# Grouped instance norm: stores of two units, gamma spread in small copies, and 1/std times gamma on ScalarE

## The chip, the cores and the metric

The kernel runs on one core of a Trainium2 chip. The metric is device time in microseconds (us). Before the change it is 626.83 us, the median of three runs (626.78 to 626.91).

## The reference, cut to what matters

```python
def reference(x, gamma):            # x: (4, 8, 16, 256, 256) f32, gamma: (8, 16) f32
    mu = x.mean(axis=(3, 4), keepdims=True)
    var = ((x - mu) ** 2).mean(axis=(3, 4), keepdims=True)
    x_norm = (x - mu) / np.sqrt(var + 1e-5)
    return x_norm * gamma[None, :, :, None, None]
```

Each of the 512 channels (4 x 8 x 16) is normalised over its own 256 x 256 plane and multiplied by one number of gamma. The input is 134.2 MB and the output as much; every byte is read once and written once.

## The kernel before

**Units.** The 512 channels are cut into `U = 32` units of `K = 16` channels. One channel's plane lies on `S = 8` partitions, so a unit is a tile of 128 partitions x 8192 f32: 32 KB on a partition, 4 MB in all. In DRAM a unit is one contiguous piece of 4 MB (`xv[u]`, `ov[u]`). Gamma has 128 numbers, so unit u takes group `u % NG` of `NG = 8` groups of 16.

**Buffers.** There are `AHEAD = 6` slots of 4 MB, each its own tile, which is nearly all of the on-chip memory. A unit is loaded into its slot, normalised in place and stored from it. Unit u+6 takes the slot of unit u, so its load waits until the store of unit u has landed.

**Queues.** The first six loads are issued at once: units 1 and 3 by ScalarE's queue (ACTq), the others by SyncE's (SPq). After that SPq issues every load (L48) and ACTq every store (L129); GpSimd's queue brings gamma's 512 bytes. An instruction waits in its own engine's order: a store issued by ScalarE stands behind ScalarE's work for that unit and ahead of its work for the next.

**Gamma, once.** One VectorE copy (L78) writes gamma, each number 8 times, into a row of 1024 numbers (`g_rep`) on one partition. Eight matmuls with a 1x1 one (L83) turn each 128 of them into a column of PSUM (`g_ps`), and one VectorE copy (L89) brings the 128 x 8 result to `g_col`. All of it stands ahead of unit 0 on VectorE.

**A unit.** The loop is written out by hand and the order on each engine is the order of the text (`manual_schedule`):

- VectorE sums the tile (L102) while ScalarE squares and sums it (L103) into the other half of `st[:, u]`.
- TensorE (L111) adds up the 8 partitions of each channel and gives the negative means to all of them, in PSUM.
- VectorE works out the negative variance (L112); ScalarE takes the root (L116); VectorE takes the reciprocal (L120) and multiplies it by gamma's column (L122).
- VectorE writes `(x - mean) * scale` over the tile (L125).
- ScalarE issues the store (L129), SyncE the load of unit u+6 (L48), which waits for that store.

Of the kernel before, what the change touches and what calls it, by code (L numbers as in the profile page):

```python
# [1 line left out]

# [4 lines left out]

F32 = mybir.dt.float32
U8 = mybir.dt.uint8
ALU = mybir.AluOpType  # L10
ACTF = mybir.ActivationFunctionType
AX = mybir.AxisListType


@with_exitstack
def kernel(
    ctx: ExitStack,
    tc: tile.TileContext,
    x: bass.AP,
    gamma: bass.AP,  # L20
    out: bass.AP,
):
    nc = tc.nc
    B, G, C, H, W = x.shape
    P = nc.NUM_PARTITIONS
    HW = H * W
    n_ch = B * G * C
    S = 8
    K = P // S
    F = HW // S  # L30
    U = n_ch // K
    NG = (G * C) // K
    AHEAD = 6
    assert HW % S == 0 and (G * C) % K == 0

    xv = x.rearrange("b g c h w -> (b g c h w)").rearrange("(u p f) -> u p f", p=P, f=F)
    ov = out.rearrange("b g c h w -> (b g c h w)").rearrange("(u p f) -> u p f", p=P, f=F)
    gv = gamma.rearrange("g c -> (g c)")

    data = ctx.enter_context(tc.tile_pool(name="data", bufs=1))  # L40
    singles = ctx.enter_context(tc.tile_pool(name="singles", bufs=1))
    psum = ctx.enter_context(tc.tile_pool(name="psum", bufs=4, space=bass.MemoryType.PSUM))
    ctx.enter_context(tc.manual_schedule())

    slots = [data.tile([P, F], F32, name=f"xt{i}") for i in range(AHEAD)]

    def load(u, queue):
        queue.dma_start(out=slots[u % AHEAD][:], in_=xv[u])  # L48


    g_row = singles.tile([1, G * C], F32, name="g_row")
    nc.gpsimd.dma_start(out=g_row[:], in_=gv[None, :])  # L52
    for u in range(AHEAD):
        load(u, nc.scalar if u in (1, 3) else nc.sync)


    eps_t = singles.tile([P, 1], F32, name="eps_t")
    nc.gpsimd.memset(eps_t[:], 1e-5)  # L58
    one = singles.tile([1, 1], F32, name="one")
    nc.gpsimd.memset(one[:], 1.0)  # L60
    navg = singles.tile([P, K, S], F32, name="navg")
    nc.gpsimd.memset(navg[:], -1.0 / HW)  # L62
    nc.gpsimd.affine_select(  # L63
        out=navg[:], in_=navg[:], pattern=[[-S, K], [0, S]], compare_op=ALU.is_ge,
        fill=0.0, base=0, channel_multiplier=1,
    )
    nc.gpsimd.affine_select(  # L67
        out=navg[:], in_=navg[:], pattern=[[S, K], [0, S]], compare_op=ALU.is_ge,
        fill=0.0, base=S - 1, channel_multiplier=-1,
    )  # L70
    navg_w = navg[:].rearrange("p k s -> p (k s)")
    root_eps = singles.tile([P, 1], F32, name="root_eps")
    nc.scalar.activation(out=root_eps[:], in_=eps_t[:], func=ACTF.Sqrt)  # L73
    g_rep = singles.tile([1, NG, K, S], F32, name="g_rep")
    g_ps = psum.tile([P, NG], F32, name="g_ps", bufs=1)
    g_col = singles.tile([P, NG], F32, name="g_col")

    nc.vector.tensor_copy(  # L78
        out=g_rep[:],
        in_=g_row[:].rearrange("o (n k) -> o n k", n=NG).unsqueeze(3).to_broadcast([1, NG, K, S]),  # L80
    )
    for n in range(NG):
        nc.tensor.matmul(  # L83
            out=g_ps[:, n : n + 1],
            lhsT=g_rep[:, n].rearrange("o k s -> o (k s)"),
            rhs=one[:],
            start=True, stop=True,
        )
    nc.vector.tensor_copy(out=g_col[:], in_=g_ps[:])  # L89

    junk = singles.tile([P, F], U8, name="junk")

    st = singles.tile([P, U, 2], F32, name="st")
    nvar = singles.tile([P, U], F32, name="nvar")
    std = singles.tile([P, U], F32, name="std")
    rstd = singles.tile([P, U], F32, name="rstd")
    scale = singles.tile([P, U], F32, name="scale")

    squares = []
    for u in range(U):  # L100
        t = slots[u % AHEAD]
        nc.vector.reduce_sum(out=st[:, u, 0:1], in_=t[:], axis=AX.X)  # L102
        square = nc.scalar.activation(  # L103
            out=junk[:], in_=t[:], func=ACTF.Square, accum_out=st[:, u, 1:2],
        )
        if u:

            tc.declare_no_dep(square.ins, squares[-1].ins, reason="junk, ordered by the root between")
        squares.append(square)
        ps = psum.tile([P, 2], F32, name="ps")  # L110
        nc.tensor.matmul(out=ps[:], lhsT=navg_w, rhs=st[:, u], start=True, stop=True)  # L111
        nc.vector.tensor_scalar(  # L112
            out=nvar[:, u : u + 1], in0=ps[:, 0:1], scalar1=ps[:, 0:1],
            scalar2=ps[:, 1:2], op0=ALU.mult, op1=ALU.add,
        )
        nc.scalar.activation(  # L116
            out=std[:, u : u + 1], in_=nvar[:, u : u + 1], func=ACTF.Sqrt,
            bias=eps_t[:], scale=-1.0,
        )
        nc.vector.reciprocal(out=rstd[:, u : u + 1], in_=std[:, u : u + 1])  # L120
        g = u % NG
        nc.vector.tensor_mul(  # L122
            out=scale[:, u : u + 1], in0=rstd[:, u : u + 1], in1=g_col[:, g : g + 1],
        )
        nc.vector.tensor_scalar(  # L125
            out=t[:], in0=t[:], scalar1=ps[:, 0:1], scalar2=scale[:, u : u + 1],
            op0=ALU.add, op1=ALU.mult,
        )
        nc.scalar.dma_start(out=ov[u], in_=t[:])  # L129
        if u + AHEAD < U:  # L130
            load(u + AHEAD, nc.sync)


# [1 line left out]
_INS = ['x', 'gamma']  # L135
_OUTS = [((4, 8, 16, 256, 256), 'float32')]


# [23 lines left out]
```

## Time and profile before

| what | value |
|---|---|
| median of three runs | 626.83 us |
| span of the profiled execution, first to last instruction | 625.2 us |
| around the span (median less span) | 1.6 us |
| bytes moved | 268.46 MB at a mean of 429 GB/s |
| DMA engines' share of the span, both queues (52.9% + 46.8%) | 99.7% |
| VectorE busy | 443.2 us (71%) |
| ScalarE busy | 238.8 us (38%) |
| TensorE busy | 21.4 us (3%) |
| granted TensorE clock | 1.000 |

The profiled execution's own time is its span with what lies around it. No time of its own is listed beside the span, so the median stands for it. Queue q1 holds the loads that SPq issues, q10 all that ACTq issues (two loads and all stores). A DMA packet of x is one row of 32 KB on one of 16 DMA engines; a unit is 8 packets on each engine.

### The profile page before, as it was taken

What the parts mean: (1) busy time and instruction counts of PE and PEld (TensorE: products, weight loads), DVE (VectorE), ACT (ScalarE), POOL (GpSimd) and SP (SyncE); (2) the same over time, 40 slices, a digit from 0 to 9 for tenths busy, and PEclk for the clock granted to TensorE, in tenths of its full rate; (3) what the DMA queues carried; (4) which work ended last, traced back from release to release, by engine and by line L of the source; (5) the groups of instructions that cost most, each with busy time, mean ns of one, the idle gap of its engine ahead of it and who ended that gap; (6) DMA issues with size and microseconds to landing.
All of it is one profiled execution on the core that took longest, in us unless ns stands there. A gap on an engine that the chain in (4) does not pass through costs nothing.

```text
span 625.2 us, 627 instructions
## 1 busy us (share of the span) xinstructions
PE 21.4 (3%) x80; PEld 19.6 (3%) x80; DVE 443.2 (71%) x162; ACT 238.8 (38%) x98; POOL 1.9 (0%) x10
## 2 busy tenths in 40 slices
PE   2000000000000000000000000000000000000000
PEld 2000000000000000000000000000000000000000
DVE  0588999999776687666786767867668676687730
ACT  0444444444443244432344423444224442244400
POOL 1000000000000000000000000000000000000000
DMA  8999999999999999999999999999999999999998
GB/s 369 436 403 436 436 436 436 436 426 432 434 434 436 424 434 436 436 434 436 436 421 434 434 434 432 432 434 436 436 434 436 436 419 434 434 436 432 432 434 369
DMA packets 9251, 268.46 MB, mean 429 GB/s; under 512 B 1057, under 2 KB 1057, under 8 KB 1057
## 3 DMA queue, kind: packets, MB, share of 16 engines
q10 hardware_dynamic: 4896, 142.61, 52.9%
q1 hardware_dynamic: 4320, 125.83, 46.8%
q14 instruction: 3, 0.02, 0.0%
q0 software_dynamic: 32, 0.00, 0.0%
HBM read 134.22 MB, written 134.22 MB: 429 GB/s over the span
## 4 chain that ended last, share of the span: by engine, by line
another core or an unknown queue 61%; DMA 17%; DVE 15%; SPq 1%; PE 1%; issue 0%; ACT 0%
DMA xt<-in_x_dram 10%; DVE st L102 10%; DMA out_dram<-xt 8%; DVE xt L125 5%; SPq L48 1%; PE ps L111 1%; ACT std L116 0%; DVE nvar L112 0%; DVE rstd L120 0%; DVE scale L122 0%
## 5 line engine op out<-in xcount | busy, mean ns | idle before, releaser
L102 DVE TENSOR_REDUCE st<-xt 128x1 f32<-128x8192 f32 x32 | 277.9, 8684 | 105.3 <-DMA xt<-in_x_dram 105.3
L103 ACT ACTIVATE junk<-xt 128x8192 uint8<-128x8192 f32 x32 | 224.9, 7029 | 275.4 <-DMA xt<-in_x_dram 232.2
L125 DVE TENSOR_SCALAR xt<-xt,ps,scale 128x8192 f32<-128x8192 f32 x32 | 145.6, 4550 | 1.2
L116 ACT ACTIVATE std<-nvar,eps_t 128x1 f32<-128x1 f32 x32 | 9.4, 294 | 79.7 <-DVE nvar L112 79.7
L111 PE MATMUL ps<-st,navg 128*128 128x2 f32 x64 | 17.9, 349 | 562.0 <-DVE st L102 562.0
L111 PEld LDWEIGHTS ps<-st,navg 128*128 128x128 f32 x64 | 16.1, 312 | 563.8 <-issue 563.8
L112 DVE TENSOR_SCALAR nvar<-ps 128x1 f32<-128x1 f32 x32 | 9.2, 287 | 23.9 <-PE ps L111 23.9
L120 DVE RECIPROCAL rstd<-std 128x1 f32<-128x1 f32 x32 | 5.3, 164 | 11.6 <-ACT std L116 11.6
L78 DVE COPY g_rep<-g_row 1x1024 f32<-1x1024 f32 x1 | 0.7, 683 | 10.6 <-DMA g_row<-in_gamma_dram 10.6
L103 ACT ACTIVATION_READ_ACCUMULATOR junk<-xt 128x1 f32 x32 | 6.0, 186 | 0.0
L122 DVE TENSOR_TENSOR scale<-rstd,g_col 128x1 f32<-128x1 f32 x32 | 5.1, 159 | 1.1
L83 PE MATMUL g_ps<-one,g_rep 1*128 1x1 f32 x16 | 3.5, 347 | 11.5 <-DVE g_rep L78 11.5
L83 PEld LDWEIGHTS g_ps<-one,g_rep 1*128 1x128 f32 x16 | 3.5, 326 | 11.4 <-issue 11.4
L89 DVE COPY g_col<-g_ps 128x8 f32<-128x8 f32 x1 | 0.2, 167 | 3.7 <-PE g_ps L83 3.7
L73 ACT ACT_TABLE_LOAD x1 | 1.3, 1283 | 1.7 <-PEq L146 1.7
L52 POOL DMA_DIRECT2D g_row<-in_gamma_dram x1 | 0.6, 607 | 0.8 <-POOLq L146 0.8
L63 POOL TENSOR_SCALAR_AFFINE_SELECT navg<-navg 128x128 f32<-128x128 f32 x1 | 0.4, 398 | 0.1
L67 POOL TENSOR_SCALAR_AFFINE_SELECT navg<-navg 128x128 f32<-128x128 f32 x1 | 0.4, 398 | 0.1
L62 POOL MEMSET navg<- 128x128 f32 x1 | 0.2, 230 | 0.0
L73 ACT ACTIVATE root_eps<-eps_t 128x1 f32<-128x1 f32 x1 | 0.2, 203 | 0.0
L58 POOL MEMSET eps_t<- 128x1 f32 x1 | 0.1, 118 | 0.0
L146 POOL MEMSET const-bfloat16-1.0<- 128x1 bf16 x1 | 0.1, 102 | 0.0
(4 smaller groups left out, 0.4 us busy)
## 6 DMA issues: line engine op xcount, KB each, us to landing
out_dram<-xt ACTq DMA_DIRECT2D x32, 4096.0 KB, 62.5
xt<-in_x_dram SPq DMA_DIRECT2D x30, 4096.0 KB, 38.5
xt<-in_x_dram ACTq DMA_DIRECT2D x2, 4096.0 KB, 31.8
g_row<-in_gamma_dram POOLq DMA_DIRECT2D x1, 0.5 KB, 9.3
```

Source lines behind the costliest of these rows:

```text
L48: queue.dma_start(out=slots[u % AHEAD][:], in_=xv[u])
L73: nc.scalar.activation(out=root_eps[:], in_=eps_t[:], func=ACTF.Sqrt)
L78: nc.vector.tensor_copy(out=g_rep[:], in_=g_row[:].rearrange("o (n k) -> o n k", n=NG).unsqueeze(3).to_broadcast([1, NG, K, S]),)
L83: nc.tensor.matmul(out=g_ps[:, n : n + 1], lhsT=g_rep[:, n].rearrange("o k s -> o (k s)"), rhs=one[:], start=True, stop=True,)
L102: nc.vector.reduce_sum(out=st[:, u, 0:1], in_=t[:], axis=AX.X)
L103: square = nc.scalar.activation(out=junk[:], in_=t[:], func=ACTF.Square, accum_out=st[:, u, 1:2],)
L111: nc.tensor.matmul(out=ps[:], lhsT=navg_w, rhs=st[:, u], start=True, stop=True)
L112: nc.vector.tensor_scalar(out=nvar[:, u : u + 1], in0=ps[:, 0:1], scalar1=ps[:, 0:1], scalar2=ps[:, 1:2], op0=ALU.mult, op1=ALU.add,)
L116: nc.scalar.activation(out=std[:, u : u + 1], in_=nvar[:, u : u + 1], func=ACTF.Sqrt, bias=eps_t[:], scale=-1.0,)
L120: nc.vector.reciprocal(out=rstd[:, u : u + 1], in_=std[:, u : u + 1])
L122: nc.vector.tensor_mul(out=scale[:, u : u + 1], in0=rstd[:, u : u + 1], in1=g_col[:, g : g + 1],)
L125: nc.vector.tensor_scalar(out=t[:], in0=t[:], scalar1=ps[:, 0:1], scalar2=scale[:, u : u + 1], op0=ALU.add, op1=ALU.mult,)
```

## The change

Three things are changed.

1. The six slots become three tiles of two units each (`pairs`); a slot is a half of one. Nothing is stored after an even unit. After an odd unit one DMA stores both units of the pair (8 MB), and then both loads of the units six later are issued. Units 30 and 31 are stored one by one. The first six loads are as before.
2. Gamma's spread is made by 32 VectorE copies of 4 numbers each (32 written), four ahead of each of the eight matmuls, and `g_col` is filled by eight copies of one column in place of one of eight columns: 40 copies in all.
3. 1/std times gamma is a ScalarE activation (`Copy` with gamma's column as its scale) in place of VectorE's multiply.

```diff
-    slots = [data.tile([P, F], F32, name=f"xt{i}") for i in range(AHEAD)]
+    pairs = [data.tile([P, 2, F], F32, name=f"xt{i}") for i in range(AHEAD // 2)]
+
+    def slot(u):
+        return pairs[u // 2 % (AHEAD // 2)][:, u % 2]
 
     def load(u, queue):
-        queue.dma_start(out=slots[u % AHEAD][:], in_=xv[u])
+        queue.dma_start(out=slot(u), in_=xv[u])
...
-    nc.vector.tensor_copy(
-        out=g_rep[:],
-        in_=g_row[:].rearrange("o (n k) -> o n k", n=NG).unsqueeze(3).to_broadcast([1, NG, K, S]),
-    )
+    g_nk = g_row[:].rearrange("o (n k) -> o n k", n=NG)
+    KQ = K // 4
     for n in range(NG):
+        for q in range(4):
+            ks = slice(q * KQ, (q + 1) * KQ)
+            nc.vector.tensor_copy(
+                out=g_rep[:, n, ks], in_=g_nk[:, n, ks].unsqueeze(2).to_broadcast([1, KQ, S]),
+            )
         nc.tensor.matmul(
...
-    nc.vector.tensor_copy(out=g_col[:], in_=g_ps[:])
+    for n in range(NG):
+        nc.vector.tensor_copy(out=g_col[:, n : n + 1], in_=g_ps[:, n : n + 1])
...
-        nc.vector.tensor_mul(
-            out=scale[:, u : u + 1], in0=rstd[:, u : u + 1], in1=g_col[:, g : g + 1],
+        nc.scalar.activation(
+            out=scale[:, u : u + 1], in_=rstd[:, u : u + 1], func=ACTF.Copy, scale=g_col[:, g : g + 1],
         )
...
-        nc.scalar.dma_start(out=ov[u], in_=t[:])
-        if u + AHEAD < U:
-            load(u + AHEAD, nc.sync)
+        if u >= U - 2:
+            nc.scalar.dma_start(out=ov[u], in_=t)
+        elif u % 2:
+            nc.scalar.dma_start(
+                out=ov[u - 1 : u + 1].rearrange("u p f -> p u f"), in_=pairs[u // 2 % (AHEAD // 2)][:],
+            )
+            for v in (u - 1 + AHEAD, u + AHEAD):
+                if v < U:
+                    load(v, nc.sync)
```

## The prediction

> **What bounds the kernel now.** First I read the slices of the page and its DMA queues.
>
> ```profile
> DMA  8999999999999999999999999999999999999998
> GB/s 369 436 403 436 436 436 436 436 426 432 434 434 436 424 434 436 436 434 436 436 421 434 434 434 432 432 434 436 436 434 436 436 419 434 434 436 432 432 434 369
> ...
> q10 hardware_dynamic: 4896, 142.61, 52.9%
> q1 hardware_dynamic: 4320, 125.83, 46.8%
> ```
>
> No slice but the first and last is under 403 GB/s, and the two queues fill 52.9 + 46.8 = 99.7% of the engines' span. The DMA engines are the bound from end to end. What can be won is what they don't do: 0.3% of 625.2, or 1.9 us, and whatever the slower slices hide. What can be lost is any moment in which both queues are empty. So the question is not what an instruction costs but whether the two queues run dry together.
>
> Next the lists of waits, VectorE's line from all engines' and SPq's from its own (total, times, longest).
>
> ```profile
> DVE st L102 <- DMA xt<-in_x_dram: 105.3, 24, 7.5
> ...
> SPq L48 <- DMA out_dram<-xt: 534.7, 26, 59.8
> ```
>
> VectorE stands 105.3 us waiting for loads, and SPq 534.7 us waiting for stores, in 26 waits: loads are released by stores, and nothing else. Then the timeline, start and length in us.
>
> ```profile
> 0.81 1.90 SPq L48 DMA_DIRECT2D xt<-in_x_dram  x4
> ...
> 10.64 0.68 DVE L78 COPY g_rep<-g_row 1x1024 f32<-1x1024 f32 x1 [10.64 <-DMA g_row<-in_gamma_dram]
> ...
> 15.05 0.17 DVE L89 COPY g_col<-g_ps 128x8 f32<-128x8 f32 x1 [3.73 <-PE g_ps L83]
> ...
> 22.76 8.69 DVE L102 TENSOR_REDUCE st<-xt 128x1 f32<-128x8192 f32 x1 [7.55 <-DMA xt<-in_x_dram]
> ...
> 32.52 0.29 ACT L116 ACTIVATE std<-nvar,eps_t 128x1 f32<-128x1 f32 x1 [2.63 <-DVE nvar L112]
> 32.84 0.17 DVE L120 RECIPROCAL rstd<-std 128x1 f32<-128x1 f32 x1 [0.36 <-ACT std L116]
> 33.04 0.16 DVE L122 TENSOR_TENSOR scale<-rstd,g_col 128x1 f32<-128x1 f32 x1
> ...
> 37.82 0.35 ACTq L129 DMA_DIRECT2D out_dram<-xt  x1
> ...
> 52.76 0.35 ACTq L129 DMA_DIRECT2D out_dram<-xt  x1
> ...
> 62.62 0.33 SPq L48 DMA_DIRECT2D xt<-in_x_dram  x1
> ...
> 81.96 0.33 SPq L48 DMA_DIRECT2D xt<-in_x_dram  x1
> ```
>
> Stores 0 and 1 are issued at 37.82 and 52.76, so a unit takes VectorE 14.93 us while it has data. Loads 6 and 7 are issued 19.34 us apart, one store and one load each: 9.68 us of DMA time for a unit alone, 19.36 when the other queue shares the engines. The order of the end is: store lands, load is issued, load queues behind an earlier load. That last queueing is the cushion, and it is what the change touches.
>
> **The change part by part.**
>
> *Forty copies ahead of unit 0.* They start with gamma at 10.64. A spread copy writes 32 numbers; L122 and L89 give 0.16 to 0.17 us for small VectorE work, and L120 to L122 start 0.20 apart. So 32 x 0.20 = 6.4; the last matmul, 0.35 by its row and some 0.25 of hand-over, 0.6; 8 x 0.20 = 1.6. VectorE is free at 10.64 + 8.6 = 19.2, and unit 0's data is there at 22.76: cost nothing, 3.5 us to spare. At 0.30 each it is 23.2 and unit 0 starts 0.5 late. Below, a start up to some 7 us late is still free, so both ends are nothing.
>
> *ScalarE multiplies.* VectorE's multiply (0.20 with its gap) goes; a trip to ScalarE comes. The trip for the root leaves VectorE idle 0.36, with 0.29 of it ScalarE; the small activation at L73 took 0.20. So +0.07 to +0.16 a unit, 0.16 taken, as L116 also has a pointer operand: 15.09 a unit, at most 5 us on VectorE in all, inside its 105.3 us of waiting. Nothing is queued behind it on ScalarE but the store, which waits for L125 anyway, and the next square, which for odd units now starts 4.5 us earlier since no store stands between. Cost nothing. If Copy made ScalarE swap tables, the only load of one in the trace is 1.28 us; two per unit would be a rival.
>
> *Pair stores.* Bytes and 32 KB rows stay. Fifteen issues of 0.34 us fall away from ACTq, which is off the path; fifteen sets of completion writes are 0.1 us at the most. What moves is time: the first store is issued after unit 1, not 0, and loads 6 and 7 wait for all 8 MB. I lay the queues out from the start.
>
> The first slice moved 369 of 436 GB/s: 15.63 x (1 - 369/436) = 2.40 us lost, 0.81 of it ahead of the first issue. So from an issue into empty queues to full rate costs 1.59. As the first store begins the stretch from 38 to 58 us runs at 413 GB/s (374, then 452 in its halves) against 433: 0.9 lost.
>
> - Store (0,1) is issued at 52.76 + 2 x 0.16 = 53.1 and flows at 54. The six loads alone last until 2.40 + 6 x 9.68 = 60.5, so the queues aren't empty. This is the 6 to 7 us of room for a late unit 0.
> - Eight units are then moved at 2.40 + 8 x 9.68 + 0.9 = 80.7, and that is when store (0,1) ends, with no load behind it: all six are done.
> - Store (2,3) needs unit 3: 22.76 + 4 x 15.09 = 83.1, flowing at 84. It is too late by some 3 us.
> - So at 80.7 both queues are dry. Store 0's last packet ends at 62.03 in the trace's packet records, its load is issued at 62.62: 0.6. With 1.59 to full rate the hole is 2.2 us.
> - From 82.3 to 84 loads 6 and 7 run alone, then share with store (2,3), which ends at 80.7 + 2.2 + 38.7 = 121.6. Store (4,5) was issued at 22.76 + 6 x 15.09 = 113.3: 8 us of room. Store (6,7) is issued at 143.5 and wanted at about 159: 15 us. In the steady state loads are issued as a store ends, the second lands 39 to 40 us later, its unit is done 15 later, and its store is wanted 77 us after the issue: 22 us of room.
> - At the end loads 30 and 31 share 38.7 us with store (26,27); store (28,29) then covers 19.4 us, store 30 another 9.7, and unit 31 needs 16. No hole.
>
> Sum on the profiled span: 625.2 + 2.2 - 0.1 = 627.3, and 1.6 around it, which brings the span to the median: **628.9 us**. The hole has bounds: 1.6 (0.6, and 1.0 from first issue to first packet, no slow start) and 3.3 (until store (2,3) flows anyway).
>
> **A rule against the trace.** A load issued at 62.62 queues with no gap behind the one in flight, so a transfer's fixed cost is hidden and fifteen fewer save 0.1. The Trainium skill, "DMA: Bandwidth & Descriptors", Anatomy of one DMA, puts about 2.0 us of fixed cost on every DMA; in series, fifteen fewer would give 30 us and a time near 599, under what 99.7% busy engines leave open. The same page, Latency and other measured facts, speaks against the change: rows a multiple of 4 MiB apart ran at 103 GB/s against 207, and a pair store steps 4 MiB between its two rows; at half rate the 30 paired units would add some 290 us, giving 918. No row here shows that step; the 16 engines stay 256 KB apart as now, so the sum doesn't take it.
>
> **The rivals.**
>
> 1. *Not slower: the hole is paid for.* The 0.9 us at the first store comes from it cutting in among fresh loads at 40 us; if at 54 it doesn't recur, the net is 2.2 - 0.1 - 0.9 = 1.2, 628.0. The hole at its low bound gives 628.3. It decides below 1.25 us. For it: I can't say what slowed those packets. Against: every first store has to cut in.
> 2. *Stores take two turns.* A pair is 64 KB contiguous on a partition; if a packet became 64 KB, stores would get two thirds of the engines. The first hole stays; at the end load 31 is thinned out, lands some 22 us after store (28,29) begins, its store flows 38.8 after that, and stores (28,29) and 30 are done at 36.4: 2.4 more, 631.3. Against: DRAM rows stay 32 KB.
> 3. *Table swaps.* 2 x 1.28 a unit makes 17.7: stores (2,3), (4,5) and (6,7) are issued at 93, 129 and 164 and wanted at 81, 122 and 163: three holes, 3 x 2.2 = 6.6, 633.3. Against: Square and Root share the one table load in the trace.
> 4. *Faster.* If the dips in the middle slices (together 131 GB/s short of 436, 4.7 us) were the stores' doing and went, it would be 4.7 - 2.1 = 2.6 faster, 624.2. Against: five large dips, thirty-two stores.
>
> **How the numbers follow.** One hole as laid out 0.62; rival 1 0.21; rival 2 0.07; rival 3 0.04; rival 4 0.03; another loss (a dependency between a pair's halves) 0.03. Measured differences under 0.2%, 1.25 us, are no change. Slower 0.62 + 0.07 + 0.04 + 0.03 = 0.76, same 0.21, faster 0.03. The forecast's own range is 628.1 to 630.0; with most of rival 1 and with rival 2 it is 627.6 to 631.4.
>
> **What would show it.** VectorE reaches unit 0 at 22.76 with copies ended by 20; the ACTq stores at 53, 83, 113; SPq issues loads 6 and 7 together near 81.3; the stretch from 80 to 84 us is the one with a dip in GB/s, with no second one; only one table load. It is wrong if store (2,3) is issued before 80, if holes recur later, or if packets change in size or rate.

## The result and the profile after

The changed kernel takes 642.25 us (median of four runs, 640.69 to 643.19) against 626.81 us: a ratio of 1.0242, 95% interval 1.0228 to 1.0255. It is 15.4 us slower where 2.1 were forecast, and outside the range. The profiled execution has a span of 639.6 us, 14.4 more than before. Times from here on are medians of all executions of a run; ratios leave out an execution that took over 1.5% longer than the fastest of the same kernel.

The slices and queues of the page, after:

```profile
DMA  9999989999999999999999999999999999999997
GB/s 379 439 427 406 441 332 428 428 422 426 426 443 410 447 400 432 443 430 428 430 426 432 416 434 430 430 424 420 428 420 428 432 428 428 414 428 412 432 400 305
...
q10 hardware_dynamic: 4656, 142.61, 51.9%
q1 hardware_dynamic: 4320, 125.83, 46.9%
```

The sixth slice (80 to 96 us, 332 GB/s) holds the hole that was forecast. But most later slices are also short of their counterparts: 400 to 430 in place of 432 to 436, and the last is 305 in place of 369. The engines' share is still 98.8%, so most of the time was lost while packets were in flight, not between them. The packet records of the trace divide it. A packet of 32 KB takes 1.213 us when undisturbed; what the packets took beyond that, summed over all and divided by 16 engines, is 1.6 us before and 10.6 after, so 9.0 of the 14.4 us is slow packets. Of the 10.6 us, 6.6 fall after the first 170 us, where the kernel before has 0.06. Moments with an engine empty give 2.0 us at 81 to 84 and 2.3 us ahead of the last store. The last 1.2 us is at the very end: the engines finish the last store up to 2.1 us apart, 1.0 before, and so stand idle for 3.0 of the last 6 us, 1.8 before.

The small edits, in the page's groups:

```profile
L132 DVE TENSOR_SCALAR xt<-xt,ps,scale 128x8192 f32<-128x8192 f32 x32 | 145.6, 4551 | 11.6 <-ACT scale L129 11.6
...
L129 ACT ACTIVATE scale<-rstd,g_col 128x1 f32<-128x1 f32 x32 | 9.4, 294 | 7.4 <-DVE rstd L127 7.4
L86 DVE COPY g_rep<-g_row 1x32 f32<-1x32 f32 x32 | 2.8, 162 | 10.6 <-DMA g_row<-in_gamma_dram 10.6
...
L76 ACT ACT_TABLE_LOAD x1 | 1.3, 1283 | 1.7 <-PEq L159 1.7
```

ScalarE's multiply takes 0.294 us and keeps VectorE idle for 11.6 / 32 = 0.36, as the root does; there is still one table load. The 32 spread copies keep VectorE busy for 2.8 us in all: they overlap, at 0.09 us from one to the next.

The timeline, start and length, at the first stores and at the last:

```profile
52.95 0.40 ACTq L139 DMA_DIRECT2D out_dram<-xt  x1
...
81.88 0.80 SPq L51 DMA_DIRECT2D xt<-in_x_dram  x2
...
83.09 0.40 ACTq L139 DMA_DIRECT2D out_dram<-xt  x1
...
113.22 0.38 ACTq L139 DMA_DIRECT2D out_dram<-xt  x1
...
349.80 0.38 ACTq L139 DMA_DIRECT2D out_dram<-xt  x1
...
428.68 0.38 ACTq L139 DMA_DIRECT2D out_dram<-xt  x1
...
610.33 8.69 DVE L109 TENSOR_REDUCE st<-xt 128x1 f32<-128x8192 f32 x1 [5.65 <-DMA xt<-in_x_dram]
...
625.52 0.35 ACTq L137 DMA_DIRECT2D out_dram<-xt  x1
```

Up to 83 us this is the schedule of the prediction within 1.2 us: stores at 52.95 and 83.09 for 53.1 and 83.1, loads 6 and 7 at 81.88 for 81.3. Later it isn't. Call a store's **room** the time that it has to spare: from its issue to the last packet of the store ahead of it in the same queue. In kernel before it settles at 42.7 us. In kernel after it is, from store (4,5) on, 11.0, 13.9, 9.6, 6.7, 4.7, 3.4, 0.9, 2.6, 0.8, 4.1, 2.7, 4.6, 3.1. It was expected near 22 and constant. A store that is issued into an empty or nearly empty queue while loads flow also waits 3.5 to 4.9 us from issue to its first packet, so at 350 and 428 us the store queue is empty for some 3 us and the loads run alone. The last unit's load lands late, its store is issued at 625.52, and the engines wait for it.

### The profile page after: what moved, and what is told of

Same layout as the page of the kernel before. It is cut to its first block, busy times and chain, and to the rows that moved or that the text cites. A ratio compares the mean times of both kernels' runs of the same rounds, so it can differ in the third digit from the quotient of the medians.

```text
span 639.6 us, 625 instructions
## 1 busy us (share of the span) xinstructions
PE 21.4 (3%) x80; PEld 19.5 (3%) x80; DVE 440.8 (69%) x168; ACT 247.8 (39%) x130; POOL 1.9 (0%) x10
## 4 chain that ended last, share of the span: by engine, by line
DMA 59%; DVE 27%; another core or an unknown queue 9%; PE 1%; ACT 1%; issue 1%; SPq 0%
DMA xt<-in_x_dram 32%; DMA out_dram<-xt 27%; DVE st L109 18%; DVE xt L132 9%; PE ps L118 1%; DVE nvar L119 1%; ACT std L123 1%; ACT scale L129 1%; DVE rstd L127 0%; SPq L51 0%
## 5 line engine op out<-in xcount | busy, mean ns | idle before, releaser
L132 DVE TENSOR_SCALAR xt<-xt,ps,scale 128x8192 f32<-128x8192 f32 x32 | 145.6, 4551 | 11.6 <-ACT scale L129 11.6
L127 DVE RECIPROCAL rstd<-std 128x1 f32<-128x1 f32 x32 | 5.2, 164 | 11.6 <-ACT std L123 11.6
L129 ACT ACTIVATE scale<-rstd,g_col 128x1 f32<-128x1 f32 x32 | 9.4, 294 | 7.4 <-DVE rstd L127 7.4
L86 DVE COPY g_rep<-g_row 1x32 f32<-1x32 f32 x32 | 2.8, 162 | 10.6 <-DMA g_row<-in_gamma_dram 10.6
```

What stands on the lines that cost most here:

```text
L86: nc.vector.tensor_copy(out=g_rep[:, n, ks], in_=g_nk[:, n, ks].unsqueeze(2).to_broadcast([1, KQ, S]),)
L129: nc.scalar.activation(out=scale[:, u : u + 1], in_=rstd[:, u : u + 1], func=ACTF.Copy, scale=g_col[:, g : g + 1],)
L132: nc.vector.tensor_scalar(out=t, in0=t, scalar1=ps[:, 0:1], scalar2=scale[:, u : u + 1], op0=ALU.add, op1=ALU.mult,)
```

## The experiments

Each time stands with its ratio to kernel before, run on the same chip, and the 95% interval. Diffs are against kernel after unless said.

**1. The small edits, and the pair stores by themselves.** The first run is kernel before with the 40 copies and ScalarE's multiply:

> Kernel before with only the 40 gamma copies and ScalarE's multiply; every unit stored by itself as before. Theory A (the 8 MB store itself: a DMA of 256 rows takes 3.6 to 4.9 us from issue to first packet and slows the loads around its start) and theory B (the grouping by pairs leaves the stores no room, so their queue runs dry, whatever the size of a store) both say no change: 626.8, within 0.5. Theory C (ScalarE's multiply or the copies carry part of the loss) says at least 628.

Measured: 627.08 us, 0.9999 (0.999 to 1.0009). The second is kernel after with gamma's copies and VectorE's multiply as before:

> Kernel after with gamma's single copies and VectorE's multiply put back; only the pair stores remain. A and B: the whole loss stays, 641 to 643. C: at least 2 us less, under 640.

Measured: 641.48 us, 1.0218 (1.0189 to 1.0246). Its runs go from 638.44 to 642.86, so within their spread the whole loss is the pair stores', and theory C is out.

**2. The same grouping in stores of 4 MB.**

```diff
-            nc.scalar.dma_start(
-                out=ov[u - 1 : u + 1].rearrange("u p f -> p u f"), in_=pairs[u // 2 % (AHEAD // 2)][:],
-            )
+            for v in (u, u - 1):
+                nc.scalar.dma_start(out=ov[v], in_=slot(v))
```

> Kernel after, but a pair leaves in two DMAs of 4 MB, one unit each, issued back to back after the odd unit; the odd unit goes first, so both loads still wait until all 8 MB have landed. Same grouping, same release, other form of the DMA. A: first packet within 1 us of issue where the queue is dry, few slow load packets, only the hole at 80 us and a small one at the end: 628 to 631. B: the grouping is unchanged, so the time stays at 639 to 643.

Measured: 631.38 us, 1.0063 (1.0048 to 1.0078). The next run has `for v in (u - 1, u)`:

> As the run with two 4 MB stores, but the even unit goes first, so its load is released when its own 4 MB have landed, not after 8 MB. A: the hole at 80 us goes as well, 627 to 628. B: the stores still come in pairs after the odd unit, but loads come earlier: part of the loss goes, 630 to 638.

Measured: 628.62 us, 1.0024 (1.0015 to 1.0034). So 10.9 of the 15.4 us belong to the form of the store, 2.8 to the release of the loads after 8 MB in place of 4, and 1.7 to issuing in pairs. In the second of the two runs the first store of a pair is also issued 5 us earlier (47.91 for 52.94), which the 2.8 takes in. With joint release the page's slices are:

```profile
DMA  8999989999999999999999999999999999999998
GB/s 369 433 432 419 433 331 433 433 417 433 433 433 434 433 433 433 433 433 433 433 433 433 433 433 433 433 433 433 433 433 433 433 433 433 433 433 433 433 433 367
```

The hole is there (331, the engines empty for 2.3 us), but from the tenth slice on every one but the last moves 433 or 434. The stores' room settles at 13.4 us and stays there. Theory A, near in its time (it gave at most 631), was wrong in its mechanism: the first packet of a 4 MB store into an empty queue took 4.59 and 5.10 us here, as long as that of 8 MB.

**3. What in the form?** Two DMAs of 4 MB by columns; two by partitions; one of 8 MB with 64 KB in one piece of DRAM; and, on kernel before, a single store in two rows per partition:

```diff
+            for h in range(2):
+                cs = slice(h * F // 2, (h + 1) * F // 2)
+                nc.scalar.dma_start(
+                    out=ov[u - 1 : u + 1, :, cs].rearrange("u p f -> p u f"),
+                    in_=pairs[u // 2 % (AHEAD // 2)][:, :, cs],
+                )
```

> Kernel after, but a pair leaves in two DMAs of 4 MB, each one half of the columns of both units: 256 rows of 16 KB each, rows of the two units 4 MB apart in DRAM. Both loads wait for both, as in kernel after. The joint two-unit run (631.4) has the release but neither the rows nor the shape. If the harm is the 8 MB in one DMA: 631. If it is the 256 rows, or the two units' rows mixed in one DMA: 638 to 643, with slow load packets at every pair.

Measured: 632.58 us, 1.0089 (1.0072 to 1.0106), near the first alternative. Slow load packets after 170 us sum to 0.02 us.

```diff
+            for h in range(2):
+                hp = slice(h * P // 2, (h + 1) * P // 2)
+                nc.scalar.dma_start(
+                    out=ov[u - 1 : u + 1, hp].rearrange("u p f -> p u f"),
+                    in_=pairs[u // 2 % (AHEAD // 2)][hp],
+                )
```

> Kernel after, but a pair leaves in two DMAs of 4 MB, each 64 partitions of both units: 128 rows of 32 KB, two units' rows mixed, 4 MB apart in DRAM. If the harm is 8 MB in one DMA, or 256 rows in one: 631. If it is the two units' rows in one DMA: 638 to 643.

Measured: 718.92 us, 1.1361 (1.1336 to 1.1386), outside both. This run has a bound of its own. Between 72 and 100 us only stores flow, and the queues in that window are:

```profile
DMA packets 217, 6.06 MB, mean 217 GB/s; under 512 B 32, under 2 KB 32, under 8 KB 32
## 3 DMA queue, kind: packets, MB, share of 16 engines
q10 hardware_dynamic: 217, 6.06, 99.5%
```

Half the partitions move at half of 433 GB/s, so the run tells nothing on rows or units.

```diff
+            nc.scalar.dma_start(
+                out=ov[u - 1 : u + 1].rearrange("u p f -> (u p f)").rearrange("(p v f) -> p v f", v=2, f=F),
+                in_=pairs[u // 2 % (AHEAD // 2)][:],
+            )
```

> Kernel after, still one DMA of 8 MB per pair after the odd unit and the same release, but each partition's two rows are written side by side in DRAM, 64 KB in one piece; so most rows of the output are in other places than the reference has them. All else is as in kernel after. If the harm is 8 MB in one DMA: 640 to 643, as after. If it is the number of rows or the jump of 4 MB between a partition's two rows: 630 to 632, as with two 4 MB stores released jointly.

Measured: 675.36 us, 1.0783 (1.073 to 1.0837). It tested something else than was meant. The rows merged into packets of 64 KB with a median of 2.42 us, so that a store's turn moved twice a load's. That is the prediction's second rival made true; it costs 48.5 us, not 4.5.

```diff
-        nc.scalar.dma_start(out=ov[u], in_=t[:])
+        nc.scalar.dma_start(
+            out=ov[u].rearrange("p f -> (p f)").rearrange("(h p f) -> p h f", h=2, p=P),
+            in_=t[:].rearrange("p (h f) -> p h f", h=2),
+        )
```

> Kernel before, one store of 4 MB per unit, released singly, but each partition's 32 KB are written as two rows of 16 KB that lie 2 MB apart in DRAM; so the rows of the output are in other places than the reference has them. 256 rows in two strides, with all the room of the kernel before (a store waits 43 us in its queue). If the harm comes from the two-stride store alone: slow load packets at every store, 630 to 650. If it needs the queue to run dry, or 8 MB: 626.8 to 627.5.

Measured: 635.73 us, 1.0142 (1.0122 to 1.0161). Inside the first alternative, but not by its mechanism: with 16 KB packets the loads get two thirds of the engines. The medians to landing are, for stores and loads of this run,

```profile
out_dram<-xt ACTq DMA_DIRECT2D x32, 4096.0 KB, 77.4
xt<-in_x_dram SPq DMA_DIRECT2D x30, 4096.0 KB, 19.4
```

against 62.5 and 38.5 before, its slow packets sum to 2.9 us, and its last slice moves 227 GB/s. What the size of a packet does to the shares had hidden what the shape does.

**4. One DMA or two, with equal rows; room; and four small stores.** The first is one DMA of 8 MB in 16 KB rows:

```diff
+                out=ov[u - 1 : u + 1].rearrange("u p f -> (u p f)").rearrange("(r p f) -> p r f", r=4, p=P),
+                in_=pairs[u // 2 % (AHEAD // 2)][:].rearrange("p u (h f) -> p (u h) f", h=2),
```

> Kernel after, still one DMA of 8 MB per pair, but in 512 rows of 16 KB that step 2 MB in DRAM, so rows of the output are in other places than the reference has them. It differs from the column halves (632.6) in that the 8 MB are one DMA and not two. A2 (one DMA of 8 MB): 638 to 645. If what counts is that a load's packet gets as large a turn as a store's or larger, and the column halves were spared by their 16 KB rows: 632 to 634.

Measured: 632.47 us, 1.0086 (1.0071 to 1.0101), as with two DMAs in such rows. In rows of 16 KB, then, a DMA of 8 MB isn't harmful as such, and theory A2 falls. The room settles at 27 us here, though, and no later store comes near an empty queue, so rows of 32 KB with little room are left to run 5.

The second shortens a unit (`t[:, 0 : F // 4]` in both sums):

> Kernel after, with both sums of a unit (VectorE's and ScalarE's) taken over a quarter of the columns, so the output is not the reference's; all DMAs as in kernel after. A unit takes VectorE about 8.6 us in place of 15.1, so store (2,3) is issued near 57 us and no queue is empty at 80, and every later store is issued some 6 us or more earlier. Theory D (the queue of stores runs dry at each pair, and a store that starts into a dry queue slows the loads): with that room the slow packets go and the time is 626 to 630. Theory A2 (the DMA of 8 MB itself disturbs the loads wherever it takes over from the one before): only the two holes go, 4 to 5 us, and 636 to 639 stays.

Measured: 635.74 us, 1.0119 (1.0077 to 1.0161), with single runs from 631.1 to 644.8: between the two, and inconclusive by its time. Its profile, of an execution of 631.59 us, says more. Although the sums take a quarter of their time, the room still falls, from 23 us by way of 15.1, 11.8, 10.1, 7.7, 6.2 and 3.8 to 1.4. Meanwhile the loads' room, counted the same way in their own queue, grows from 10.5 to 22.9. So the compute isn't what uses it up: the loads fall behind the stores. And from 200 us on, with stores starting into an empty queue at every other pair or so, there are no slow packets to speak of (0.05 us). An empty queue alone doesn't slow the loads, and theory D falls too, as far as this execution shows; the slower ones have no profile.

The third is kernel before with `AHEAD = 4`:

> Kernel before with four slots in place of six, all else the same: single 4 MB stores, one load released by each. A store waited 42.7 us in its queue before; with two units less in flight that falls by 38.7 to about 4 us, as little as in kernel after. Theory D (a queue near dry slows the loads, whatever the store): slow packets at most units, 10 us or more, 637 and above. A2 (8 MB in one DMA): the loads stay at full rate, 627 to 630.

Measured: 631.47 us, 1.0064 (1.0049 to 1.0079). The room didn't fall to 4 us but to 14, where it stayed constant for 25 units with next to no slow packets (0.2 us after 170 us); the loss is two empty moments, 1.5 us at 52 and 2.3 at the end, and 1.8 us more of slow packets than in kernel before, nearly all in the first 170 us. It doesn't test D as meant.

The fourth has the two-unit loop of run 2 with each store cut into two column halves:

> Kernel after, but a pair leaves in four DMAs of 2 MB (half the columns of one unit, 128 rows of 16 KB), the odd unit first, so both loads wait for all as in kernel after. It has the 16 KB rows of the column halves (632.6) and the unmixed units of the two 4 MB stores (631.4). If 16 KB rows cost the 1.2 us between those two: 632.6. If mixing two units in one DMA costs it: 631.4. Under 640 in any case, since no DMA is 8 MB.

Measured: 645.65 us, 1.0279 (1.0243 to 1.0316), a miss. TensorE's waits (total, times, longest), which in kernel after end with VectorE's sum, name the cause:

```profile
PE ps L118 <- ACT junk L110: 339.1, 15, 28.5
```

and so does ScalarE's timeline:

```profile
146.69 15.52 ACTq L142 DMA_DIRECT2D out_dram<-xt  x4
162.26 7.03 ACT L110 ACTIVATE junk<-xt 128x8192 uint8<-128x8192 f32 x1 [20.19 <-issue]
```

Eight semaphores go round among the DMAs. With six DMAs a pair a store needs the semaphore of a load that hasn't landed; ScalarE's queue needs up to 15 us for the four issues, and the next square stands behind them. In the lines above the second store waits until 159.26 us for the semaphore of load 9, which landed at 159.24. The run tells nothing on the form of a store.

**5. Turns.** The packet records can be put in order for each of the 16 engines. `S6+7.3` is the fourth packet of the store of units 6 and 7, `L10.0` the first of load 10. One engine in kernel before, the two 4 MB stores with joint release (where unit 7 goes ahead of 6), and kernel after:

```
before  S13.6 L17.7 S13.7 L18.0 S14.0 L18.1 S14.1 L18.2 S14.2 L18.3 S14.3
2x4 MB  L10.3 S7.7 L10.4 L10.5 S6.0 L10.6 S6.1 L10.7 S6.2 S6.3 L11.0 S6.4
after   L9.7 S6+7.4 S6+7.5 L10.0 S6+7.6 ... L10.7 S6+7.13 S6+7.14 L11.0 S6+7.15 L11.1 L11.2 S8+9.0
```

The queues alternate packet by packet, except where a DMA ends: after its last packet that queue misses a turn and the other goes twice (`S6+7.4 S6+7.5` after load 9's last packet, `L11.1 L11.2` after the store's). The turn goes to the completion write, which the records show in that place (4 bytes, 9 ns). So 4 MB take 9 turns, but 8 MB take 17. Two loads need 18 turns a pair and a pair store 17: the loads fall behind at every pair, the room of the stores wears away, and with it the constant order of the two queues. Before, and with two stores of 4 MB, both sides need 18. One turn of a queue comes round every 2 x 1.21 = 2.4 us, so by this estimate the room should fall by 2.4 us a pair; it falls by 2.6 in kernel after (13.9 to 0.9 in five pairs) and by 2.3 with the quarter sums (15.1 to 1.4 in six). Theory T, then; it can be turned round. First a DMA of 1 KB, two more turns, behind each pair store:

```diff
+    bits = singles.tile([16, U // 2, 16], F32, name="bits")
...
+            nc.scalar.dma_start(out=bits[:, u // 2], in_=xv[u, 0:16, 0:16])
```

> Theory T: on each DMA engine the two queues take turns, one packet each, and the completion of a DMA takes a turn of its queue. Loads of 4 MB need 9 turns for 8 packets, so 18 a pair; a store of 8 MB needs 17 for 16. So in kernel after the loads fall a turn or more behind the stores at every pair, until the stores have no room left and their queue runs dry. This run is kernel after with a DMA of 1 KB (16 rows of 64 bytes of x into a spare tile that nothing reads) behind every pair store on ScalarE's queue: 2 more turns, 19 against 18, and no bytes to speak of. Theory T: the stores no longer gain on the loads, their room stays at 13 us or grows, 629 to 634. If the 8 MB store harms by itself: 640 to 643, or slower for the added DMA.

Measured: 634.42 us, 1.0108 (1.0091 to 1.0125); runs of 632.8, 634.3, 634.6 and one of 646.1, which no profile explains. That is just above T's 634. An added DMA takes off 7.8 us. The page's slices:

```profile
GB/s 371 439 434 410 431 325 435 433 410 419 425 431 432 431 433 435 433 431 435 433 437 431 433 435 431 431 437 431 431 431 433 435 433 433 431 437 433 431 433 321
```

From the twelfth on all but the last are at 431 to 437. The room now grows, from 15.3 to 19.3 us, and stays. Slow packets after 170 us sum to 0.05 us, for 6.6 in kernel after. In the other direction, the same DMA behind the loads of the two-store kernel, and as a control behind its stores:

> The two 4 MB stores with joint release (631.4), which have no 8 MB DMA at all, with the same 1 KB DMA on SyncE's queue behind every pair of loads: 20 turns for the loads against 18 for the stores. Theory T: the loads fall behind by 2 turns, 2.4 us, a pair, the stores' room of 13.4 us is gone after some five pairs, and the time rises to 636 to 643 as in kernel after. If the 8 MB store harms by itself: 631 to 632.

Measured: 652.16 us, 1.041 (1.0367 to 1.0452), above both alternatives. (The expectation counts 1.2 us a turn; at the 2.4 of the estimate above, two turns are 4.8 us a pair.)

> The control: the two 4 MB stores with joint release and the 1 KB DMA on ScalarE's queue, behind the stores. Theory T: 20 turns for the stores against 18 for the loads, the loads gain, the room grows, 630 to 632. If an added small DMA costs time by itself: as much as in the run with it on SyncE's queue.

Measured: 631.57 us, 1.0071 (1.0056 to 1.0086). The two are on the sides that T says, and slow packets after 170 us sum to 11.7 us in the first and 0.06 in the second, but the pair isn't clean. With five DMAs a pair ScalarE's queue again stands for semaphores: TensorE waits for ScalarE's square 292.0 us in the first run and 293.5 in the second, and in the first run alone a wait also holds back the second store of a pair, by up to 17 us. So the 20.8 us of the first can't be put down to turns alone. In the second the stores' room didn't grow as T had it: with the units held back it settles at 5.6 to 6.8 us, down from 13.4. The loads did gain: their own room falls from 6.9 to between 0.7 and 2.1.

Last, equal turns the other way round: the quarter sums of run 4, and loads of 8 MB too, so 17 turns on both sides and no added DMA:

```diff
-            for v in (u - 1 + AHEAD, u + AHEAD):
-                if v < U:
-                    load(v, nc.sync)
+            v = u - 1 + AHEAD
+            if v < U:
+                nc.sync.dma_start(
+                    out=pairs[v // 2 % (AHEAD // 2)][:], in_=xv[v : v + 2].rearrange("u p f -> p u f"),
+                )
```

> The run with sums over a quarter of the columns (635.74, with runs from 631.1 to 644.8), and from the seventh unit on a pair is also loaded by one DMA of 8 MB: 17 turns a pair for the loads and 17 for the stores. The output is not the reference's, since the sums leave out three quarters of the columns; these cover what the later landing of the even unit costs. Theory T: with equal turns neither queue gains on the other, the stores' room stays constant from pair to pair in place of falling from 23 to 1 us, the slow load packets end early, and the time is 628 to 631 with a small spread. If DMAs of 8 MB harm by themselves: 635 or more, with as wide a spread.

Measured: 629.80 us, 1.0042 (1.0028 to 1.0056), five runs within 629.6 and 629.92, for 631.1 to 644.8 with loads of 4 MB. The room is 9.1 us at every pair from 185 us on. The slices, and the issues with the median to landing:

```profile
GB/s 370 434 416 432 430 418 432 422 434 434 432 430 434 434 431 432 434 430 430 434 434 432 434 432 434 434 434 434 434 434 434 434 432 434 434 434 434 434 432 317
...
out_dram<-xt ACTq DMA_DIRECT2D x15, 8192.0 KB, 49.7
xt<-in_x_dram SPq DMA_DIRECT2D x13, 8192.0 KB, 48.9
```

The same store of 8 MB, beside loads that take as many turns, keeps its place. Unequal turns are what makes the room wear away: shown by the order of the packets, by the cure with added turns and by this run. One link is open. The slow packets (mostly loads, up to 2.9 us in place of 1.213) come above all where a store starts: of the 6.6 us after 170 us in kernel after, 4.9 lie between 1.5 us ahead of a store's first packet and 5 us behind it. They come while the ends of the two queues' DMAs move against each other, and are absent (at most 0.2 us after 170 us) in all kernels whose order has settled; what in the memory or the engines slows them was not found, and the run with quarter sums and 4 MB loads has stretches with neither a settled room nor slow packets.

## Why the prediction was wrong

**Right:** what bounds the kernel, and what to ask (do both queues run dry together). The small edits cost nothing: 19.2 us was forecast for the end of gamma's work and it came at 15.4, since small copies overlap, and a unit takes 15.07 us for 15.09. The first store's cut into the loads, 0.9, measured 0.86, so the first rival, in which it doesn't recur, fails. The hole: forecast at 80.7 with 2.2 us, it came at 81.5 with 2.0. That schedule, made from the rows of before, held to 1.2 us for the first 83.

**Wrong, the step that failed:** "fifteen sets of completion writes are 0.1 us at the most". They were priced by their duration, and 9 ns each, as the packet records have it, is right as time on an engine. Their price is the turn. The kernel before hides this, since both queues have DMAs of 4 MB and miss as many turns; no wait and no group shows it. The Trainium skill, "DMA: Bandwidth & Descriptors", Anatomy of one DMA, calls the semaphore's write "essentially free", in a section on DMAs that GpSimd issues (the 2.0 us of fixed cost that the prediction takes from it are measured on those too). For the DMAs of SyncE and ScalarE here the 9 ns agree, but the write also lets the other queue go once more, 1.21 us.

**What hung on it.** "22 us of room" in the steady state was worked out with equal halves for both queues; the first store of that state, (8,9), has 9.6, which wears away to 1 to 4. Turns are only one part of this, for with equal turns, in the two 4 MB stores, the room is constant but 13.4. The other part is "the second lands 39 to 40 us later", which takes the load queue to be empty at the issue. In that run a pair's first load is issued 6.9 us before the load ahead of it is done, and the second's last packet ends 45.6 us after the issue (160.00 to 205.65): the two queues share the room, 13.4 + 6.9 = 20.3. The loads were late from the start: a load issued into an empty queue while a store flows took 4.4 us to its first packet in kernel after (load 8, 124.66 to 129.09), where 1.0 was taken from the first issue, into idle engines. "At the end ... No hole" fell for the same reason: the last load came late and 2.3 us were lost. The 9.0 us of slow packets have no term in the sum; the 0.9 at the first store was taken as one event, and the trace has 0.0 to 0.9 us of it around the first packet of every pair store, 7.1 us over the fifteen.

**The rivals.** That stores take another share of the turns than loads was there as the second rival, by a packet of 64 KB; the share was off by one turn in 18 and not by two to one. Where a packet did become 64 KB it cost ten times what the rival said. The loss at a row pitch of 4 MiB, which the prediction cites from the same page and leaves out of its sum, doesn't show here: the last run has that step between a partition's two rows, in its loads and stores, and moves 432 to 434 GB/s in its settled slices. Faster and table swaps were rightly put low.

Of the 14.4 us between the spans: hole 2.0, the wait for the last store 2.3, slow packets 9.0, and the uneven finish 1.2, to within rounding.

## What to carry to other kernels

The two DMA queues here took turns by packets, and every completion was a turn: for queues that are meant to run in step count turns, not bytes, and keep sizes of rows and DMAs equal on both sides. Joining transfers on one queue alone moves the balance, and the loss hardly showed in busy shares (98.8% for 99.7%); look at each queue's room over time, by the issues and landings. When several DMAs are split off or added, look also at how many a cycle there are: with more than four a pair here the issuing engine stood waiting for semaphores in use.

## What the runs showed of the hardware

- A queue that has run empty gets its first packet 3.4 to 5.6 us after the issue while the other queue flows (2.7 to 2.9 where the other was only just issued too), and 0.85 to 1.0 us after it when the other is idle or nearly done. The size of the DMA (4 or 8 MB) makes no clear difference.
- Stores from 64 partitions alone moved 217 GB/s, half of 433.
- Merging two rows of 32 KB into one packet of 64 KB took the kernel from 642.25 to 675.36 us, with as many bytes moved; the rows also went to other places.
